# Entry of the second mixture, clock keepers, router banks, GpSimd's queue and two orders of block 3 in a three-block transformer kernel

## The chip, the cores and the metric

The kernel runs on one core of a Trainium2 chip. It is one program that computes three transformer blocks in a row. What counts is its time on the device in microseconds, as the median of several runs. TensorE (PE) runs at one of two clock levels, 1.2 and 2.4 GHz; the profile shows the granted clock of a stretch as a share of the full one, so 0.50 is the lower level throughout. The other engines are VectorE (DVE), ScalarE (ACT), GpSimd (POOL) and SyncE (SP); transfers are issued from the queues of SP, ACT and POOL.

## What is computed

All activations are 512 rows of 1024 (S = 512, D = 1024), fp32. The reference, cut to the parts that the change touches:

```
x = first_block(x, mem, ...)        # mixer, cross attention, small mixture
# second block
merged = g0 * (o_da @ w_da_o) + g1 * (o_wa @ w_wa_o) + g2 * (o_xa @ w_xa_o)
x  = x + merged @ w_out
h2 = rmsnorm(x, ffn_norm_g)
aff  = softmax(h2 @ w_router)                    # 512 x 16
g, i = top_k(aff.T, 64)                          # each expert takes 64 rows
xe   = h2[i]
ye   = (silu(xe @ w_gate) * (xe @ w_up)) @ w_down * g    # 16 experts of 2048
x    = x + scatter_add(ye, i)
x    = rmsnorm(x, final_norm_g)
# third block
q, k, v, q_lat, kv_lat, k_rope, g_a, g_b = split(x @ w_in)
y_a = neighbourhood_attention_2d(q, k, v, rpb) @ w_branch_na    # 8 rows of 64 columns
y_b = latent_attention(q_lat, kv_lat, k_rope, ...) @ w_branch_mla
m   = (sigmoid(g_a) * y_a + sigmoid(g_b) * y_b) @ w_out
x   = layer_norm(a * x + m); x = layer_norm(a * x + swiglu(x))
```

## The kernel before, in words

The rows of the activations are four tiles of 128 (a = 0 to 3). Dense products of fp32 operands are made from two halves each: `split` (L227 on ScalarE, L230 on VectorE) makes wh and wl from the raw weights, and each pair of tiles takes three products (high-high, high-low, low-high). The order on each engine is fixed when the program is built: a scheduler places the instructions by their due times, and `issue_after` ties some to others. TensorE runs its row strictly in that order. PSUM has four banks called acc, two called pst, and one pair of banks called sc; a product waits until the earlier reader of its bank is done.

**The second block's end.** Four gatings of the last branch (L1320, L1321) write kv on VectorE and GpSimd. Then `out_proj` (L291) multiplies merged by w_out, in two passes over pairs of tiles, (0, 1) and (2, 3), each with four acc banks. Ahead of it, h is loaded again from memory by four transfers on ScalarE's queue (L1587). When a pair is done, `add_h` (L320) adds to h, and for each tile `moe2_tile` runs: the rows are normed (L901, L905), transposed (L442) and copied, and `router` (L912) makes 16 logits, in the sc bank. Exp (L1615) reads them there; then a transposition (L1619) brings the probabilities into aff, 16 rows of 512.

**The second mixture's entry.** Eight rounds of MAX8 and MATCH_REPLACE8 on VectorE (L1632, L1633) pick 64 rows for each expert. After each, `keep_warm` lets TensorE multiply the eight maxima (L200) and then, in the first six rounds, three times the 128-column identity (L202). A scan (L1639) turns the picks into positions pos, which are transposed (L1645) and compared with a row of indices to a one-hot oh (L1656). `gather` (L1664) multiplies xh by oh, k by k for the first pair of experts. Each expert then multiplies its 64 rows by the gate and up weights (L1701), transposes the result (L1726) and multiplies by the down weights (L1738). For each pair of experts, four spreading products (L1708, two instructions each in the trace) copy the pair's rows of pos and aff over the partitions, from which the scatter matrix is made. The weights arrive by SP's queue, 1 MB each, into a ring of buffers; a transfer waits until the products that read its buffer before are done. Some of the first up weights go to other rooms (L1680).

**Block 3.** The dense product of V (L376) is copied out by VectorE (L1810), written to memory (vd, L1811) and read back as eight windows vw (L1830); rv, the position biases, are read by L1839. All of these stand on ScalarE's queue. Then Q and K follow (L428), the neighbourhood attention with its value products (L1876), and the latent attention, `mla_part`: for each pair of heads, transposes of Q and K (L1961), and then four parts of 128 rows each, with two scores products (L1968), a softmax (ScalarE L477, VectorE L485), transposes of e (L442), copies eT by VectorE (L445) and ScalarE (L447), and value products (L1980). `stagger` interleaves the parts: each part's scores are issued one or two parts ahead of its transposes and values.

## Time and profile before

| | us |
|---|---|
| median of three runs | 3352.58 |
| the runs | 3346.15 to 3354.76 |
| the profiled execution | 3355.08 |
| its span, first to last instruction | 3353.2 |

The span is 1.9 us shorter than the profiled execution; durations are taken from this execution. The mean granted clock is 0.983. TensorE is busy for 94% of the span, VectorE 49%, ScalarE 39%, GpSimd 4%. The stages, roughly: 0 to 900 us the first block, 900 to 1525 the second block's mixer, 1525 to 1575 its output projection, 1575 to 1612 the mixture's entry, 1612 to 2540 the sixteen experts, then block 3: V, Q and K to 2630, the neighbourhood attention to 2720, its branch and the latents to 2807, the latent attention to 2881, and the feed-forward to the end. A row of a timeline shows the start, the length, the engine and its operation, xcount where equal ones follow each other, and in brackets the idle time ahead of it with what ended it.

### The profile page before, as it was taken

Reading aid. Unit: us, or ns where it says so; the run is one execution under the profiler, and the core shown is the slowest. Engines: PE = TensorE matmul, PEld = TensorE weight load, DVE = VectorE, ACT = ScalarE, POOL = GpSimd, SP = SyncE. Lnnn points to the kernel's source line nnn. Section 1 sums busy time; section 2 is a strip of 40 time slices with the busy share of each in tenths; the row PEclk is TensorE's granted clock in tenths of the full one; section 3 lists DMA queues with packets and bytes.
Section 4 is the critical chain, followed back from the end, with each engine's and each line's share of the span. In section 5 each row is a group of like instructions: output and inputs, shape, how many; then the busy total and the mean of one; then the engine's idle time right before and its main releaser. Section 6 shows DMA issues by size and latency. Waiting matters only on the chain.

```text
span 3353.2 us, 41283 instructions
## 1 busy us (share of the span) xinstructions
PE 3168.3 (94%) x15456; PEld 2062.4 (62%) x15456; DVE 1632.4 (49%) x3520; ACT 1291.2 (39%) x2662; POOL 130.9 (4%) x128
## 2 busy tenths in 40 slices
PE   8999989998989999999999999899888999999998
PEld 6778766667758777677534333322225685788886
DVE  5557799987364444856211111011105546573356
ACT  6335568876354354654000000000003444452244
POOL 0010110001000000000000000000000000000000
PEclk9999989999999999999899999999999999999999
DMA  5115489975112122125799999999995220132243
GB/s 174 67 66 157 173 305 382 370 282 177 63 38 88 63 66 88 39 89 199 315 420 426 427 427 427 427 427 427 427 427 205 72 95 26 63 114 90 81 170 138
DMA packets 196554, 713.96 MB, mean 213 GB/s; under 512 B 20144, under 2 KB 28096, under 8 KB 147584
## 3 DMA queue, kind: packets, MB, share of 16 engines
q1 hardware_dynamic: 173888, 668.38, 51.4%
q10 hardware_dynamic: 19520, 32.43, 3.1%
q0 software_dynamic: 2944, 10.49, 1.0%
q8 instruction: 123, 2.02, 0.2%
q14 instruction: 79, 0.65, 0.1%
HBM read 693.68 MB, written 17.56 MB: 212 GB/s over the span
## 4 chain that ended last, share of the span: by engine, by line
PE 69%; DMA 15%; DVE 8%; ACT 4%; issue 2%; POOL 1%; ACTq 0%; POOLq 0%; SPq 0%; DVEq 0%
PE acc L428 23%; PE acc L291 7%; PE acc L1701 6%; PE acc L1103 5%; PE acc L1295 5%; DMA xl<-in_w_exp_up_dram 3%; DMA rawx<-in_w_exp_gate_dram 3%; PE acc L1738 3%; PE acc L1125 3%; DMA rawx<-in_w_exp_down_dram 2%; DMA xl<-in_w_exp_down_dram 2%; PE sc L1664 2%; PE acc L376 2%; PE pst L442 2%; DVE wl L230 2%
## 5 line engine op out<-in xcount | busy, mean ns | idle before, releaser
L230 DVE TENSOR_TENSOR wl<-raw,wh 128x512 fp32r<-128x512 f32 (+3 forms) x910 | 606.0, 682 | 578.6 <-ACT wh L227 528.9
L227 ACT CAST wh<-raw 128x512 fp32r<-128x512 f32 (+3 forms) x910 | 546.5, 612 | 717.1 <-PE acc L428 475.1
L428 PE MATMUL acc<-xh,wh 128*128 128x512 f32 x1072 | 426.5, 398 | 7.2 <-ACT wh L227 5.2
L428 PE MATMUL acc<-xl,wh 128*128 128x512 f32 x1072 | 424.5, 396 | 0.0
L428 PE MATMUL acc<-xh,wl 128*128 128x512 f32 x1072 | 423.1, 395 | 0.0
L1701 PE MATMUL acc<-rawx,xe 128*64 128x512 f32 x1256 | 293.1, 601 | 28.1 <-DMA rawx<-in_w_exp_up_dram 20.4
L428 PEld LDWEIGHTS acc<-xh,wh 128*128 128x128 f32 x1072 | 202.4, 189 | 57.1 <-ACT wh L227 7.8
L428 PEld LDWEIGHTS acc<-xh,wl 128*128 128x128 f32 x1072 | 202.5, 189 | 47.0 <-issue 6.7
L428 PEld LDWEIGHTS acc<-xl,wh 128*128 128x128 f32 x1072 | 202.7, 189 | 44.2 <-issue 5.6
L1701 PEld LDWEIGHTS acc<-rawx,xe 128*64 128x64 f32 x1256 | 84.4, 137 | 227.5 <-issue 149.8
L1738 PE MATMUL acc<-rawx,wh 128*64 128x512 f32 x640 | 145.9, 598 | 10.6 <-DMA rawx<-in_w_exp_down_dram 10.6
L291 PE MATMUL acc<-wl,xsh 128*128 128x512 f32 x336 | 133.8, 398 | 4.8 <-DVE wl L230 4.7
L216 POOL TENSOR_TENSOR pw_r<-pw_v,halfneg 128x1 f32<-128x1 f32 (+2 forms) x64 | 59.1, 924 | 2008.2 <-DVE pw_v L215 1990.6
L291 PE MATMUL acc<-wh,xsl 128*128 128x512 f32 x336 | 132.9, 396 | 0.0
L291 PE MATMUL acc<-wh,xsh 128*128 128x512 f32 x336 | 128.9, 392 | 0.0
L1701 PE MATMUL acc<-raw,xe 128*64 128x512 f32 x512 | 118.5, 597 | 8.4 <-DMA raw<-in_w_exp_gate_dram 8.4
L1720 DVE SCALAR_TENSOR_TENSOR wl<-wl,acc 128x512 f32<-128x512 f32 x32 | 22.0, 687 | 203.6 <-PE acc L1701 203.6
L1727 ACT COPY wh<-pst 128x512 f32<-128x512 f32 x32 | 18.8, 586 | 259.8 <-PE pst L1726 259.7
L477 ACT ACTIVATE e<-e,smx 128x512 f32<-128x512 f32 (+3 forms) x160 | 98.9, 619 | 50.2 <-DVE smx L475 36.4
L1103 PE MATMUL acc<-wh,xeh 128*96 128x512 f32 x256 | 103.7, 406 | 0.7 <-ACT xeh L227 0.7
L1738 PEld LDWEIGHTS acc<-rawx,wh 128*64 128x64 f32 x640 | 42.7, 136 | 99.2 <-issue 70.7
L1103 PE MATMUL acc<-wl,xeh 128*96 128x512 f32 x256 | 103.5, 404 | 0.1
(537 smaller groups left out, 5475.1 us busy)
## 6 DMA issues: line engine op xcount, KB each, us to landing
rawx<-in_w_exp_up_dram SPq DMA_DIRECT2D x80, 1024.0 KB
rawx<-in_w_exp_down_dram SPq DMA_DIRECT2D x80, 1024.0 KB
rawx<-in_w_exp_gate_dram SPq DMA_DIRECT2D x77, 1024.0 KB
raw<-in_w_in_dram SPq DMA_DIRECT2D x58, 1024.0 KB
raw<-in_w_exp_gate_dram SPq DMA_DIRECT2D x34, 1024.0 KB
raw<-in_w_exp_down_dram SPq DMA_DIRECT2D x32, 1024.0 KB
raw<-in_w_exp_up_dram SPq DMA_DIRECT2D x30, 1024.0 KB
raw<-in_w_ffn_out_dram SPq DMA_DIRECT2D x22, 1024.0 KB
```

The costliest lines, as they stand in the source:

```text
L227: nc.scalar.copy(hi, src)
L230: nc.vector.tensor_sub(lo, src, hi.bitcast(F32))
L291: nc.tensor.matmul(acc[a, hf], l[:, js], r, start=(k == 0 and q == 0), stop=(k == nk - 1 and q == 2))
L376: self.nc.tensor.matmul(acc[a], l[:, k, js], r[:, :n], start=(k == 0 and q == 0), stop=(k == nk - 1 and q == 2))
L428: nc.tensor.matmul(outs[j], l, r, start=(kk == 0 and q == 0), stop=(kk == nk - 1 and q == 2))
L442: nc.tensor.transpose(pt[:, k * P:(k + 1) * P], src[:, (b + k) * P:(b + k + 1) * P], self.ident)
L477: nc.scalar.activation(es[i], src[i], AF.Exp, bias=nm[:, i:i + 1], scale=sc[i], accum_out=l[:, i:i + 1])
L1103: nc.tensor.matmul(ps, l[:, k], r, start=(k == 0 and q == 0), stop=(k == 7 and q == 2))
L1125: nc.tensor.matmul(py[hf], l[:, k], r, start=(k == 0 and q == 0), stop=(k == 3 and q == 2))
L1295: nc.tensor.matmul(acc[j], l[:, js], r, start=(k == 0 and q == 0), stop=(k == nk - 1 and q == 2))
L1701: nc.tensor.matmul(acc[f // 2][f % 2 * 64:(f % 2 + 1) * 64], cur[:, k, es], raw[f], start=(k == 0), stop=(k == 7))
L1738: nc.tensor.matmul(py[hf * 64:(hf + 1) * 64], uT[ab][:, kk, c * 64:(c + 1) * 64], raw[:, d, hf * 512:(hf + 1) * 512], start=(i + d == 0), ...
```

## The change

The change does the following.

- Clock keepers: `keep_busy` takes the place of `keep_warm` in the mixture's entry. Its filling products are bf16, 128 by 512, of an identity that is cast once (identb). There are four behind router 2, six behind router 3, four behind the last transposition of the probabilities, three in each of the eight top-k rounds and five at the comparison behind them. They are tied by `issue_after`.
- Router banks: with 16 columns, `router` takes an acc bank instead of sc.
- The row scaling of xs (L905) moves behind Exp in `moe2_tile`; in the first mixture it stays where it was, written in `moe1_tile`.
- The spreading products are tied behind the last product of the gate.
- The loads of h, the writes of vd and the reads of vw and rv go to GpSimd's queue.
- Block 3: V is copied into rooms of the later attention (ne, neT); the weights of V and Q are requested first, those of K go into the room of merged, which is now one tile, m.
- Latent attention: `weave` takes the place of `stagger`; the two scores products of a part are issued apart from each other, and the second, as well as the value products, is tied behind other parts' work in the last three head pairs.
- One eviction of the first mixer (fq) moves from ScalarE to VectorE.

The diff, cut to its core:

```diff
+    def keep_busy(self, x, n, behind=None):
+        ps = self.acc()
+        if x is not None:
+            behind = self.nc.tensor.matmul(ps[:, :x.shape[1]], self.ident[:16], x, start=True, stop=True).ins
+        b = self.identb[:, :P]
+        with self.tc.issue_after(behind):
+            for _ in range(n):
+                self.nc.tensor.matmul(ps, b, b.unsqueeze(1).to_broadcast([P, 4, P]), start=True, stop=True)
...
-                nc.scalar.activation(fq[j], ps, AF.Copy, scale=0.125)
+                nc.vector.tensor_scalar(fq[j], ps, 0.125, None, op0=OP.mult)
...
-        pl = self.sc()[:, 0, :n]
+        pl = self.sc()[:, 0, :n] if n == 20 else self.acc()[:, :n]
...
-            nc.scalar.dma_start(self.h[:, a], self.res_d[a * P:(a + 1) * P, :])
+            nc.gpsimd.dma_start(self.h[:, a], self.res_d[a * P:(a + 1) * P, :])
...
         pl = self.router(xt, 16)
+        if a > 1:
+            self.keep_busy(None, 2 * a, self.routed)
...
         nc.scalar.activation(L, pl, AF.Exp, scale=r, bias=st[:, 1:2], accum_out=st[:, 2:3])
+        nc.scalar.activation(self.hn[:, a], self.hn[:, a], AF.Copy, scale=r)
...
+        if a == 3:
+            self.keep_busy(None, 4, mm.ins)
...
-                self.keep_warm(m8[:16], 3 if i < 6 else 0)
+                self.keep_busy(m8[:16], 3)
...
             nc.vector.tensor_scalar(wk[:16], wk[:16], 0.0, None, op0=OP.is_lt)
+            self.keep_busy(wk[:16, :8], 5)
...
-                    for b, src in ((bp, pos), (bw, aff)):
-                        for d in range(2):
-                            nc.tensor.matmul(b[d * 64:(d + 1) * 64],
+                    with tc.issue_after(gated):
+                        for b, src in ((bp, pos), (bw, aff)):
+                            for d in range(2):
+                                nc.tensor.matmul(b[d * 64:(d + 1) * 64],
...
-            nc.scalar.dma_start(vd[a * P:(a + 1) * P, :], t)
-        self.dense_tiles(W, 8, 1024, 512, xh, xl, ev_v)
+            nc.gpsimd.dma_start(vd[a * P:(a + 1) * P, :], t)
+        raws = {c: [self.raw_group(W, kg, 4, c, 512) for kg in (0, 4)] for c in (1024, 0)}
+        for kg in (0, 4):
+            nc.sync.dma_start(room[:, kg:kg + 4], W[kg * P:(kg + 4) * P, 512:1024].rearrange("(g p) n -> p g n", p=P))
+        raws[512] = [room[:, kg:kg + 4] for kg in (0, 4)]
+        self.dense_tiles(W, 8, 1024, 512, xh, xl, ev_v, raws=raws[1024])
...
-        stagger((mla_part(hp, qt) for hp in range(1, 4) for qt in range(4)), 2)
+        weave([mla_part(hp, qt) for hp in range(1, 4) for qt in range(4)], 2, True)
```

In the changed file L301 is the product of `out_proj`, L452 the transposes, L921 the router, L212 and L208 the keepers, L1664 the transposition of pos, L1683 the gather, L1720 gate and up, L1730 the spreading products, L1748 the transposes ahead of down, L1997 the scores and L2015 the values of the latent attention, L1635 that of the probabilities.

TensorE between the two tile pairs of `out_proj`, before:

```order
L442 MATMUL pst<-c_ident,xh 128x128 x4
L912 MATMUL sc<-rw_8578,gate 128x16 x4
L291 MATMUL acc<-wl,xsh 128x512
L291 MATMUL acc<-wh,xsl 128x512
L291 MATMUL acc<-wh,xsh 128x512
L442 MATMUL pst<-c_ident,xh 128x128 x4
L291 MATMUL acc<-wl,xsh 128x512
L912 MATMUL sc<-rw_8578,gate 128x16 x4
```

The same place after:

```order
L452 MATMUL pst<-c_ident,xh 128x128 x4
L921 MATMUL acc<-rw_8578,gate 128x16 x4
L452 MATMUL pst<-c_ident,xh 128x128 x4
L921 MATMUL acc<-rw_8578,gate 128x16 x4
L452 MATMUL pst<-c_ident,xh 128x128 x8
L921 MATMUL acc<-rw_8578,gate 128x16 x4
L301 MATMUL acc<-wh,xsh 128x512
```

The products of the second pair, which stood between transposes and routers, now begin behind three half routers and all the transposes.

TensorE at the entry of the mixture, from the transposition of pos to the gate, before (names: rawx and raw are weights, xe the gathered rows):

```order
L1645 MATMUL pst<-c_ident,pos 128x16 x4
L1708 MATMUL pst<-pos,c_ident 64x512 x2
L1708 MATMUL pst<-aff,c_ident 64x512
L1664 MATMUL sc<-oh,xh 128x128 x4
L1708 MATMUL pst<-aff,c_ident 64x512
L1701 MATMUL acc<-rawx,xe 64x512 x4
L1664 MATMUL sc<-oh,xh 128x128 x4
```

The same place after, with the last keeper at its head:

```order
L212 MATMUL acc<-identb 128x512
L1664 MATMUL pst<-c_ident,pos 128x16 x4
L1683 MATMUL sc<-oh,xh 128x128 x4
L1720 MATMUL acc<-rawx,xe 64x512 x4
L1683 MATMUL sc<-oh,xh 128x128 x4
```

And where the spreading products of the first pair of experts stand after, on the same engine, behind the last products of expert 0's up weights:

```order
L1720 MATMUL acc<-yp,xe 64x512 x2
L1730 MATMUL pst<-pos,c_ident 64x512 x2
L1730 MATMUL pst<-aff,c_ident 64x512 x2
L1683 MATMUL sc<-oh,xh 128x128 x4
L1748 MATMUL pst<-c_ident,wl 128x128 x4
```

They moved from between the transposition of pos and the gate to between the up products and the transposes ahead of down.

TensorE in the latent attention, at the first part of the second head pair, before:

```order
L1968 MATMUL sc<-mkT,mqT 128x512 x2
L442 MATMUL pst<-c_ident,e 128x128 x8
L1980 MATMUL acc<-eT,mv 64x128
L1968 MATMUL acc<-mkT,mqT 128x512
L1980 MATMUL acc<-eT,mv 64x128 x7
L1968 MATMUL acc<-mkT,mqT 128x512
L442 MATMUL pst<-c_ident,e 128x128 x8
```

The same place after:

```order
L1997 MATMUL sc<-mkT,mqT 128x512
L452 MATMUL pst<-c_ident,e 128x128 x8
L1997 MATMUL sc<-mkT,mqT 128x512
L2015 MATMUL acc<-eT,mv 64x128 x8
L1997 MATMUL acc<-mkT,mqT 128x512
L452 MATMUL pst<-c_ident,e 128x128 x8
```

The second scores product of a part moved between the transposes of an older part and its value products.

## Rows read from the trace of the kernel before

**Rows 1.** Stages: window, length, busy time by engine, clock, DMA share, GB/s.

```profile
1525.00:1549.00 24.00, 23.78 (x100) 19.51 (x101) 16.86 (x29) 12.59 (x25) 0.00 (x0) 0.93 0.51 213
1592.00:1603.00 11.00, 11.00 (x43) 9.76 (x43) 10.21 (x22) 0.00 (x0) 0.00 (x0) 0.50 1.02 428
1608.00:1616.00 8.00, 8.00 (x20) 3.02 (x20) 1.04 (x2) 0.59 (x1) 0.00 (x0) 0.50 0.00 0
1612.00:1653.00 41.00, 41.00 (x196) 17.75 (x196) 5.06 (x9) 3.13 (x8) 0.00 (x0) 0.94 0.77 295
1760.00:2486.00 726.00, 673.03 (x2996) 232.45 (x2994) 91.38 (x134) 40.63 (x69) 0.00 (x0) 1.00 1.01 427
2138.00:2148.00 10.00, 7.03 (x32) 1.80 (x28) 0.49 (x1) 0.00 (x0) 0.00 (x0) 1.00 1.01 424
2820.00:2830.00 10.00, 8.80 (x33) 4.86 (x31) 4.25 (x10) 2.69 (x8) 0.00 (x0) 0.56 0.00 0
2830.00:2880.00 50.00, 43.60 (x310) 27.12 (x312) 29.15 (x62) 23.85 (x62) 0.00 (x0) 1.00 0.00 1
```

**Rows 2.** Waits of SP's queue, 1560 to 1700: total us, times, longest us.

```profile
SPq L1734 <- PE acc L1701: 43.7, 12, 24.9
```

**Rows 3.** Timeline of TensorE at the entry: start us, length us, operation.

```profile
1582.87 3.49 PE L912 MATMUL sc<-rw,gate 128*128 128x16 f32 x16 [1.39 <-ACT L L1615]
...
1604.71 1.97 PE L1708 MATMUL pst<-pos,c_ident 16*64 16x512 f32 x4
...
1608.31 2.08 PE L1664 MATMUL sc<-oh,xh 128*128 128x128 f32 x8
1610.31 1.96 PE L1708 MATMUL pst<-aff,c_ident 16*64 16x512 f32 x2
1612.21 3.68 PE L1701 MATMUL acc<-rawx,xe 128*64 128x512 f32 x8
...
1620.25 1.16 PE L1664 MATMUL sc<-oh,xh 128*128 128x128 f32 x8
```

**Rows 4.** Timeline of VectorE at the entry, first and last round of eight.

```profile
1589.09 0.68 DVE L1632 MAX8 m<-aff 16x8 f32<-16x512 f32 x1
...
1599.81 0.68 DVE L1632 MAX8 m<-nx 16x8 f32<-16x512 f32 x1
...
1605.07 0.69 DVE L1656 TENSOR_TENSOR oh<-c_iota,pn 128x512 f32<-128x512 f32 x1
```

**Rows 5.** Timeline of TensorE in the output projection.

```profile
1525.22 0.80 PE L291 MATMUL acc<-wl,xsh 128*128 128x512 f32 x1 [2.32 <-DVE wl L230]
...
1548.51 0.49 PE L291 MATMUL acc<-wl,xsh 128*128 128x512 f32 x1
...
1555.72 0.39 PE L291 MATMUL acc<-wl,xsh 128*128 128x512 f32 x1
1555.95 0.40 PE L291 MATMUL acc<-wh,xsl 128*128 128x512 f32 x1
```

**Rows 6.** GpSimd's indirect loads: durations ns min/median/max, first and last start us.

```profile
L1132 POOL DMA_INDIRECT xe<-hn_d,rt x16: 909/1313/2398, 425.8 to 636.5; - x16
```

**Rows 7.** Timeline of ScalarE at block 3's entry.

```profile
2585.51 0.62 ACT L227 CAST wh<-raw 128x512 fp32r<-128x512 f32 x1 [10.02 <-DMA vw<-vd]
```

**Rows 8.** Timeline of TensorE at the same place.

```profile
2594.37 0.80 PE L428 MATMUL acc<-xh,wh 128*128 128x512 f32 x1 [4.88 <-ACT wh L227]
...
2600.08 0.46 PE L428 MATMUL acc<-xl,wh 128*128 128x512 f32 x1
```

**Rows 9.** Transfers of GpSimd's queue: count, median us from issue to landing.

```profile
xe<-hn_d,rt POOLq DMA_INDIRECT x16, 8.2
```

**Rows 10.** The neighbourhood attention's value products: durations ns, first and last start us.

```profile
L1876 PE MATMUL pst<-neT,vw x128: 272/273/324, 2630.6 to 2684.8; 128*64 128x128 f32 x128
```

**Rows 11.** Waits of TensorE, 2800 to 2885: total us, times, longest us.

```profile
PE acc L1980 <- ACT eT L447: 7.1, 10, 0.7
```

**Rows 12.** Timeline of TensorE in the latent attention.

```profile
2847.02 1.12 PE L1968 MATMUL acc<-mkT,mqT 96*128 96x512 f32 x2
```

More of the change, by code (lines that the diff above doesn't have):

```diff
@@ L1599, in moe2_open @@
         self.aff = R.tile([P, S], F32, name="aff")
-        self.pad = R.tile([P, 72], F32, name="rpad")
+        self.identb = R.tile([P, 144], BF, name="identb")
+        nc.vector.tensor_copy(self.identb[:, :P], self.ident)
         self.hn = self.xp.tile([P, 8, S], F32R, name="xh").bitcast(F32).rearrange("p (a k) t -> p a (k t)", a=4)
@@ L1700, in moe2 @@
                         for f in range(4):
-                            nc.tensor.matmul(acc[f // 2][f % 2 * 64:(f % 2 + 1) * 64], cur[:, k, es], raw[f],
-                                             start=(k == 0), stop=(k == 7))
+                            mm = nc.tensor.matmul(acc[f // 2][f % 2 * 64:(f % 2 + 1) * 64], cur[:, k, es], raw[f],
+                                                  start=(k == 0), stop=(k == 7))
+                    if not pg:
+                        gated = mm.ins
                     pg.append(acc)
@@ L1800, in mixer3 @@
         o_ml = [B.tile([P, S], F32, name=f"oml{i}") for i in range(4)]
-        merged = [B.tile([P, S], F32, name=f"m{i}") for i in range(8)]
+        room = B.tile([P, 8, S], F32, name="m")
+        merged = [room[:, i] for i in range(8)]
         self.g8 = B
@@ L1808, in ev_v @@
         def ev_v(a, ps):
[L1809 removed]
+            t = (N.tile([P, 2, 256], F32, name="ne", bufs=2).rearrange("p i k -> p (i k)") if a % 2 else
+                 N.tile([P, 4, P], F32, name="neT", bufs=2).rearrange("p k t -> p (k t)"))
             nc.vector.tensor_copy(t, ps)
[L1811 to L1813 removed]
+            nc.gpsimd.dma_start(vd[a * P:(a + 1) * P, :], t)
[4 more added lines that the diff above has]
+        self.dense_tiles(W, 8, 1024, 512, xh, xl, ev_v, raws=raws[1024])
         anti = self.const("anti", N)
@@ L1966, in mla_part, with scores @@
             sp = self.sc() if hp == 0 or qt % 2 == 0 else [self.acc(), self.acc()]
-            for b in range(2):
-                nc.tensor.matmul(sp[b] if isinstance(sp, list) else sp[:, b], T[2 * b][:96, qt * P:(qt + 1) * P],
-                                 T[2 * b + 1][:96], start=True, stop=True)
+            def scores(b):
+                return nc.tensor.matmul(sp[b] if isinstance(sp, list) else sp[:, b],
+                                        T[2 * b][:96, qt * P:(qt + 1) * P], T[2 * b + 1][:96], start=True, stop=True)
+            scores(0)
+            yield
+            with behind():
+                last[0] = scores(1).ins
             e = H.tile([P, 2, S], F32, name="e", bufs=3)
@@ L1974, in mla_part @@
             for b in range(2):
-                self.transposes(eT[:, b], e[:, b], 4, eng="a" if b else "v")
+                last[0] = self.transposes(eT[:, b], e[:, b], 4, eng="a" if b else "v")
+            yield
             po = self.pst() if hp == 0 else self.acc()
@@ L1981, in values, with behind, weave @@
                                         start=(kt == 0), stop=(kt == 3))
-            self.together([lambda kt=kt, b=b: values(kt, b) for kt in range(4) for b in (1, 0)])
+            with behind():
+                self.together([lambda kt=kt, b=b: values(kt, b) for kt in range(4) for b in (1, 0)])
             nc.scalar.copy(o_ml[hp][:, qt * P:(qt + 1) * P], po[:, :P])
         heads = {}
-        stagger(mla_part(0, qt) for qt in range(4))
+        last = [None, False]
+        def behind():
+            return tc.issue_after(last[0]) if last[1] else ExitStack()
+        def weave(parts, depth, tied):
+            open_ = []
+            for g in parts:
+                o = open_.pop(0) if len(open_) == depth else None
+                next(g)
+                last[1] = tied and o is not None
+                if o is None or not tied:
+                    next(g)
+                if o is not None:
+                    next(o)
+                    if tied:
+                        next(g)
+                    next(o, None)
+                open_.append(g)
+            last[1] = False
+            for g in open_:
+                next(g)
+                next(g, None)
+        weave([mla_part(0, qt) for qt in range(4)], 1, False)
         for hf in range(2):
```

26 lines of the change are left out of this document (13 added, 13 removed).

## The prediction, made before the changed kernel ran

> **What bounds the kernel now.** The table by stage comes first, since one bound does not hold for the whole span [rows 1]. From 1760 to 2486 us the DMA engines are full (share 1.01, 427 GB/s) while PE works 673 of 726 us: the sixteen large experts of the second mixture are bound by their weights, so PE time saved there is worth nothing. What counts is when that stream starts to run without a break. Between 1608 and 1616 us DMA moves 0 GB/s, and PE runs at half clock (granted 0.50). In the other stages that the change touches PE is the bound: 100% busy, or waiting for one named engine.
>
> Why DMA stands still is read from the queue's own waits [rows 2]: the loads of down weights wait for products of the gate (L1701), 24.9 us at the longest. All weight buffers are full, and the first comes free only when the first eight products of the gate, begun at 1612.21, have run [rows 3]. So PE's way to that row is the path. Ahead of it stand, in PE's own row [rows 3]: the last router (L912 x16, which waits 1.39 us for a score bank that Exp still reads), the top-k rounds, and then eight spreading products (L1708), six of them from 1604.71 on, ahead of the first gather (L1664), and two behind it at 1610.31. The gather's one-hot was ready at 1605.07 + 0.69 = 1605.76 [rows 4]; the gather began at 1608.31.
>
> **The entry of the mixture.** *Spreading products behind the gate.* The gather can start 2.4 us earlier (1608.31 to about 1605.9). Between gather and gate stand 1.9 us of spreading products; PE then waits instead for the copy of the gathered tile. No row shows that wait bare; it is above 0 and not over the 1.9, since the gate followed the spreading products at once. I take half, so 1.0 us is won and 3.4 us together, at either clock. The eight instructions now stand behind the products of expert 0's up weights, still ahead of its down products; their 3.6 + 1.9 = 5.5 us, halved at full clock to 2.7, can delay the release of buffers there. The first expert has PE 41 of 41 us busy with DMA at 0.77 [rows 1], so this is not hidden; I charge 1 us (0 to 2.7), nearer to 0, because PE catches up: from 1760 on it has slack. In later pairs PE idles 53 us in 726 for weights, and the same move costs nothing.
>
> *Router banks.* The routers of 16 columns leave the score bank for an accumulator bank. The 1.39 us wait goes, but four keepers now stand there (about 0.9 us at full clock by the step below, 1.7 at half), so at best 0.5 us is won.
>
> *Keepers of full width.* The old ones are 128 columns of fp32; PE is busy 11.00 of 11 us from 1592 to 1603 and the granted clock stays at 0.50 [rows 1]. It comes back only behind the 512-column products that begin at 1612.21: the gather takes 2.08 us at 1608.31 and 1.16 at 1620.25 [rows 3]. The new keepers are 512-column products, four after router 2, ten around router 3, three in each top-k round and five after the last. A round is (1599.81 - 1589.09) / 7 = 1.53 us of VectorE [rows 4]; three keepers at full clock take 0.7 of it, with their first product some 0.9, 6 parts in 10, and from 2138 to 2148 the clock stays at 1.00 with PE busy 7.03 of 10 [rows 1]. Then the last router takes half of its 3.49 us (1.7 won), the gather 1.16 in place of 2.08, the first eight gate products about half of 3.68 (1.8) [rows 3]. With about 0.6 us of queue for the five keepers ahead of the last transpose, this is 0.5 + 1.7 + 0.9 + 1.8 - 0.6 = 4.3 us, beside the 3.4 of the order. VectorE's chain is unchanged. If the clock is not up, the keepers of a round take 1.3 us and their first product some 0.5, 0.3 more than the round; over eight rounds, with some of the last five behind, PE lags by up to 2.7 us, and the entry gains 3.4 - 2.7 to 3.4, some 1 to 3 us.
>
> By the Trainium skill, TensorE: Matmul & The Clock Gate, Part 1, section "What's actually happening", activity as such releases the throttle. The row of 1592 to 1603 us speaks against reading it plainly: full activity, half clock. By the plain rule the new keepers do no more than the old, and the sum is that of the first rival.
>
> The entry: 3.4 + 4.3 - 1 = 6.7, and I take **-7** (-10 to -1). DMA resumes by as much earlier, and the weights behind it are fixed in number.
>
> **The output projection ahead of it.** *Its start.* PE waits 2.32 us for the low half of the first weights (VectorE L230), which stands behind the last gatings; then it runs below full clock: 0.93 over 24 us [rows 1, 5], 1.7 us lost. Now the first split stands ahead of the gatings, and the loads of h leave ScalarE's queue for GpSimd's. The accumulator banks still have to be read first, one VectorE instruction on 128x512 ahead of the first (0.69 by the size of [rows 4]). I take **-3** (0 to -4). On GpSimd's queue these four loads stand between multiplications of kv, 1.31 us of issue each by GpSimd's indirect loads, the nearest row [rows 6]. That kv is the second half of the operand, which comes up after four of eight steps, some 10 us later, and h is first needed when the first pair of tiles is done, about 1548 [rows 5]: both are covered.
>
> *Its middle.* Between the tile pairs 19 products of the second pair, 1548.51 to 1555.95, fill the waits of the transposes and routers [rows 5]; one is 0.23 us, so 4.3 us of cover. With routers in accumulator banks the second pair finds its banks only after the additions to h and Exp; in the new order three routers' halves and all transposes come ahead of the first product of the second pair. PE then waits for the copies: from 0 (the rest of the chain gets shorter by as much) to 4.3 us. I take **+2.5**, nearer to the upper end, since in the new order no product is left between them.
>
> **Block 3's entry.** ScalarE's queue holds the gathers of the windowed V (vw). One of them waits for V to land, and the cast of the next weights waits 10.02 us behind it [rows 7]; PE ends up idle for 4.88 us at 2594.37, and its next 13 products step by (2600.08 - 2594.37) / 13 = 0.44 us in place of 0.23 [rows 5, 8]: 4.9 + 13 x 0.21 = 7.6 us, with a smaller wait ahead of it about 8. The change moves vd, vw and rv to GpSimd's queue, which has nothing else to do in this stage; the K weights come early into other room. What is late next is vw itself: the wait for the last V block begins at 2585.51 - 10.02 = 2575.5 [rows 7]; a write and four gathers at 1.31 us of issue and 8.2 us to land twice [rows 6, 9] are done by about 2599. Its first reader, L1876, runs at 2630.6 [rows 10], some 8 us earlier after the change, at 2622: 23 us of room. I take **-8** (-8.5 to 0).
>
> **Latent attention.** PE waits ten times, 7.1 us together, between transposes of e and their value products, for ScalarE's copy eT [rows 11]. The new order puts the second scores product of the next part there, about 1 us of work (the row of one shows 1.12 [rows 12]), against 0.7 us of wait. Eight to ten of these waits are covered; at the last two parts nothing is left to put there. Scores come later by one transposition, but the softmax has two parts' time. **-5** (-10 to +1: the low end if the stretch at half clock from 2820 to 2830 shrinks as well, the other if the reduction of the late scores holds VectorE's copy). The eviction of fq from ScalarE to VectorE in the first mixer is four instructions of the size of rows 7's cast (0.62 us) beside full PE: 0.
>
> **Sum.** -7 - 3 + 2.5 - 8 - 5 = -20.5 us. Against the profiled execution (3355.1 us, 3353.2 of it span) that is 3334.6; against the median of 3352.6 it is 3332.1. The forecast is stated on the median: **3332 us**.
>
> **Rivals.**
> *Clock stays down at the entry.* Keepers wait for each round's first product and leave gaps; the old ones did nothing for the clock. Against it: the products behind which it did come back, at the gate and at 2600.08 [rows 8], have 512 columns too. The entry gives 2 in place of 7: 3337. Chance 0.22.
> *The first expert gives it back.* PE is full to 1760 and DMA stands at 0.77 there, so buffers are released at PE's pace; with the spreading products and the middle of the projection at their upper ends (-2 and +2), and a DMA stream that only starts 3 us earlier, the second mixture nets 0: 3352.6 - 13 = 3339.6, or 3340. Chance 0.13.
> *GpSimd's queue is late.* Its indirect loads take from 0.91 to 2.40 us to issue, 1.31 at the median, beside a VectorE that works [rows 6]. Two writes and four gathers use up the 23 us of room when each takes 23 / 6 = 3.8 us more than 1.31, some 5.1 us, twice the longest seen. At 6.5 us each, vw is 8 us late, and block 3's gain is gone: 3340. Chance 0.05. The Trainium skill, SBUF — State Buffer, section "SBUF: two separate sides", gives such a mechanism: a DMA issued by GpSimd waits while VectorE runs an operation that takes the port they share; no run here shows it.
> *The attention loses the clock (slower).* At the start of the last three head pairs PE waits for scores banks, and the clock falls: 0.56 in 2820 to 2830, while the 50 us behind are at 1.00 with 43.6 us busy [rows 1]. The new order begins with the same wait. If its mix of transposes and short products does not bring the clock back at 2829, the 50 us take about 35 us more (half clock nearly doubles 43.6 us; 6.4 us of idle absorb a part). It decides itself at one point, the first part of the second head pair. Sum -15.5 + 35: 3372. Against: the waits that lie between are fewer than before. Chance 0.03.
> *The scheduler undoes it.* Row scalings still stand ahead of Exp of tile 2, and if PE's time is set by other chains in each place: 3350. Chance 0.05.
>
> **How the numbers follow.** Forecast 0.52, rivals 0.22, 0.13, 0.05, 0.03, 0.05. The range is from 3320 (all gains at their far ends: -10 - 4 + 0 - 8.5 - 10 = -32.5) to 3347: it takes in the first three rivals and leaves out the last two and the tails. About 0.3%, 10 us, is what a measurement of this kernel can tell from no change: faster means below 3342.5. The forecast and the first rival are there nearly whole, the second and third in somewhat over half: 0.83. Within 0.3%: 0.13. Slower: 0.04.
>
> **What would show it.** The first gate product starts at about 1605 in place of 1612.2, with a granted clock of 1.00 from about 1590; no stretch of 0 GB/s longer than 3 us near 1608; the spreading products stand behind the up products. PE has no wait over 1 us near 2590 and no clock below 0.9 there. The ten eT waits are down to two to four. PE idles up to 2.5 us near 1550. Wrong it would be if the expert phase ends less than 4 us earlier relative to the start of the entry, or if a wait for vw or rv shows in the neighbourhood attention.

## The result and the profile after

The changed kernel takes 3331.62 us, the median of four runs (3330.38 to 3334.32); the kernel before, on the same chip, 3352.76 us (four runs). The ratio is 0.9941, with an interval of 0.9924 to 0.9959: faster by 0.6%, 21 us. The forecast was 3332 us. The profiled execution took 3330.38 us, so it is 24.7 us shorter than the profiled one of before (3355.08).

The page of the changed kernel gives the span and the busy time of the engines.

```profile
span 3328.6 us, 41332 instructions
PE 3153.2 (95%) x15465; PEld 2052.6 (62%) x15465; DVE 1636.8 (49%) x3525; ACT 1289.8 (39%) x2658; POOL 143.5 (4%) x152
```

The same line of the page of before:

```profile
PE 3168.3 (94%) x15456; PEld 2062.4 (62%) x15456; DVE 1632.4 (49%) x3520; ACT 1291.2 (39%) x2662; POOL 130.9 (4%) x128
```

The number of products is nearly the same. TensorE's busy time falls by 15.1 us, its idle time by the other 9.5: a product at half clock counts as busy for longer, so part of what the clock costs stands in the busy time.

To see where it went, both traces are cut at the same products of TensorE, and each piece is measured from the cut before it. That is needed here: the time at which `out_proj` is reached, about 1520 us, differed by 6 us (1519.6 to 1525.6) between ten profiled executions whose instructions up to there are the same (those of the changed kernel and of all experiments but one that moved the loads of h).

| piece | forecast, us | before | after | difference |
|---|---|---|---|---|
| to the start of `out_proj` | 0 | 1522.05 | 1520.20 | -1.9 |
| its first tile pair | -3 | 26.10 | 22.91 | -3.2 |
| its rest ("middle") | +2.5 | 27.92 | 35.86 | **+7.9** |
| its end to the first product of the gate | -5.9 | 36.14 | 29.21 | -6.9 |
| first product of the gate to the last scatter product | -0.8 (-1.8 for the first eight products of the gate, +1 charged) | 930.7 | 931.3 | +0.6 |
| last scatter product to the last neighbourhood value | -8 | 141.9 | 135.9 | -6.0 |
| from there to the first acc scores of the latent attention | 0 | 126.9 | 125.8 | -1.1 |
| latent attention, to the last value product | -5 | 69.0 | 55.0 | **-14.0** |

The sum of the last column is -24.6. That is 3.6 us more than the medians differ by: the profiled execution of before lies 2.3 us above its median here, that of the changed kernel 1.2 below. Two rows are far from the forecast, and they partly cancel: the middle of `out_proj` lost 5.4 us more than was priced, and the latent attention won 9 us more. The table by stretch (length, then busy time of each engine with its instructions, then granted clock, DMA share, GB/s) shows the middle in the changed kernel:

```profile
1541.00:1543.00 2.00, 2.00 (x10) 1.37 (x8) 1.97 (x5) 0.83 (x3) 0.00 (x0) 1.00 0.00 0
1543.00:1545.00 2.00, 1.29 (x11) 1.01 (x10) 2.00 (x4) 2.00 (x4) 0.00 (x0) 1.00 0.00 0
1545.00:1547.00 2.00, 1.22 (x11) 0.98 (x11) 1.51 (x4) 2.00 (x5) 0.57 (x1) 0.98 0.03 8
1547.00:1549.00 2.00, 2.00 (x11) 2.00 (x11) 1.42 (x6) 0.58 (x1) 0.56 (x1) 0.50 0.00 0
...
1557.00:1559.00 2.00, 2.00 (x6) 1.54 (x6) 1.18 (x4) 0.52 (x3) 0.00 (x0) 0.50 0.00 0
1559.00:1561.00 2.00, 2.00 (x7) 1.41 (x6) 0.68 (x3) 1.03 (x2) 0.00 (x0) 0.61 0.00 0
```

and TensorE's timeline of the same place (start, length, operation, count, and the wait ahead of it) shows why:

```profile
1542.68 0.39 PE L301 MATMUL acc<-wh,xsl 128*128 128x512 f32 x1
1543.11 0.63 PE L452 MATMUL pst<-c_ident,xh 128*128 128x128 f32 x4
1544.41 1.07 PE L921 MATMUL acc<-rw,gate 128*128 128x16 f32 x8 [0.67 <-ACT gate L457]
1545.33 0.63 PE L452 MATMUL pst<-c_ident,xh 128*128 128x128 f32 x4
1546.74 1.75 PE L921 MATMUL acc<-rw,gate 128*128 128x16 f32 x8 [0.78 <-DVE gate L455]
...
1552.41 0.63 PE L301 MATMUL acc<-wl,xsh 128*128 128x512 f32 x1
```

In [rows 5] the products of the second pair stand between transposes and routers here. Now they are gone from there, as the forecast said, and TensorE waits 0.67 + 0.78 = 1.45 us. What it did not say: behind these waits the granted clock falls to 0.50 and stays there from 1547 to about 1560.5 us. 13.5 us at half clock are 6.7 us of lost work, and a product is 0.63 long in place of 0.39. 1.45 + 6.7 = 8.2, against 7.9 in the table.

At the entry, the same view and the same timeline answer [rows 1] and [rows 3]:

```profile
1575.00:1590.00 15.00, 12.90 (x81) 9.55 (x80) 8.41 (x23) 6.18 (x12) 1.48 (x2) 1.00 0.81 264
1590.00:1600.00 10.00, 7.25 (x33) 3.12 (x31) 9.31 (x21) 0.00 (x0) 0.00 (x0) 1.00 0.99 397
1600.00:1608.00 8.00, 5.33 (x29) 2.99 (x29) 5.93 (x12) 0.00 (x0) 0.00 (x0) 1.00 0.78 330
1608.00:1612.00 4.00, 3.82 (x10) 1.02 (x11) 0.13 (x1) 0.00 (x0) 0.00 (x0) 0.57 0.00 0
1612.00:1620.00 8.00, 8.00 (x44) 4.00 (x43) 0.29 (x1) 0.27 (x1) 0.00 (x0) 1.00 0.73 262
```

```profile
1605.18 0.41 PE L1664 MATMUL pst<-c_ident,pos 16*128 16x16 f32 x4 [0.78 <-DVE pos L1661]
1606.64 1.16 PE L1683 MATMUL sc<-oh,xh 128*128 128x128 f32 x8 [1.04 <-DVE oh L1675]
1608.18 3.55 PE L1720 MATMUL acc<-rawx,xe 128*64 128x512 f32 x8 [0.38 <-DVE xe L1687]
```

The clock is up from 1575 to 1608, the gather takes 1.16 us instead of 2.08, and no spreading product stands ahead of the gate. But TensorE then waits 0.78, 1.04 and 0.38 us, and the clock falls once more: the first eight products of the gate take 3.55 us, hardly less than the 3.68 of [rows 3], and DMA stands at 0 GB/s from 1608 to 1612.

In block 3, GpSimd's timeline shows the moved transfers: what is shown is the time of each issue on its queue.

```profile
2562.37 2.75 POOL L1858 DMA_DIRECT2D vw<-vd  x4 [2.33 <-DMA vd<-ne]
2565.11 0.59 POOL L1835 DMA_DIRECT2D vd<-neT  x1
2570.44 0.56 POOL L1835 DMA_DIRECT2D vd<-ne  x1 [4.74 <-DVE ne L1834]
2579.12 2.73 POOL L1858 DMA_DIRECT2D vw<-vd  x4 [8.12 <-DMA vd<-ne]
```

The wait for V to land is still there, 8.12 us, but nothing that TensorE needs is queued behind it. The waits of TensorE from 2530 to 2690 us (who waits for whom, total, times, longest) no longer have a row of the Q and K products; one of 1.4 us in V's products (L386), for the low half xl of the input rows, is new. In [rows 8] it was 4.88 us at one place.

```profile
PE acc L386 <- DVE xl L240: 1.4, 1, 1.4
PE pst L1769 <- DVE h L1772: 0.7, 1, 0.7
```

In the latent attention, the waits for eT, ten in [rows 11], are two:

```profile
PE acc L2015 <- ACT eT L457: 2.1, 2, 1.3
PE sc L1997 <- ACT e L488: 1.8, 1, 1.8
```

### The profile page after: what moved, and what is told of

Its sections match the earlier page's. It is cut to its first block, busy times and chain, and to the rows that moved or that the text cites. A ratio compares the mean times of both kernels' runs of the same rounds, so it can differ in the third digit from the quotient of the medians.

```text
span 3328.6 us, 41332 instructions
## 1 busy us (share of the span) xinstructions
PE 3153.2 (95%) x15465; PEld 2052.6 (62%) x15465; DVE 1636.8 (49%) x3525; ACT 1289.8 (39%) x2658; POOL 143.5 (4%) x152
## 4 chain that ended last, share of the span: by engine, by line
PE 54%; DMA 12%; DVE 6%; ACT 3%; issue 1%; POOL 1%; ACTq 0%; POOLq 0%; SPq 0%; DVEq 0%
PE acc L438 20%; PE acc L1720 8%; PE acc L301 5%; PE acc L1306 5%; PE acc L1760 4%; DMA xl<-in_w_exp_up_dram 3%; DMA rawx<-in_w_exp_gate_dram 3%; DMA xl<-in_w_exp_down_dram 3%; PE sc L1683 2%; DMA rawx<-in_w_exp_down_dram 2%; PE pst L1769 2%; ACT e L488 2%; PE pst L452 1%; DMA rawx<-in_w_exp_up_dram 1%; PE acc L386 1%
## 5 line engine op out<-in xcount | busy, mean ns | idle before, releaser
L240 DVE TENSOR_TENSOR wl<-raw,wh 128x512 fp32r<-128x512 f32 (+1 forms) x902 | 601.0, 683 | 556.7 <-ACT wh L237 507.8
L237 ACT CAST wh<-raw 128x512 fp32r<-128x512 f32 (+1 forms) x902 | 542.4, 612 | 696.3 <-PE acc L438 468.6
L1720 PE MATMUL acc<-rawx,xe 128*64 128x512 f32 x1256 | 290.3, 600 | 28.5 <-DMA rawx<-in_w_exp_up_dram 20.2
L1720 PEld LDWEIGHTS acc<-rawx,xe 128*64 128x64 f32 x1256 | 85.4, 137 | 223.5 <-issue 145.2
L301 PE MATMUL acc<-wl,xsh 128*128 128x512 f32 x336 | 133.8, 398 | 3.0 <-DVE wl L240 2.9
L301 PE MATMUL acc<-wh,xsl 128*128 128x512 f32 x336 | 133.3, 397 | 0.0
L1741 DVE SCALAR_TENSOR_TENSOR wl<-wl,acc 128x512 f32<-128x512 f32 x32 | 22.0, 688 | 223.5 <-ACT wl L1740 223.5
L1740 ACT ACTIVATE wl<-acc 128x512 f32<-128x512 f32 x32 | 19.1, 597 | 287.4 <-PE acc L1720 287.4
L301 PE MATMUL acc<-wh,xsh 128*128 128x512 f32 x336 | 130.1, 396 | 0.0
L1720 PE MATMUL acc<-raw,xe 128*64 128x512 f32 x512 | 118.8, 598 | 8.5 <-DMA raw<-in_w_exp_gate_dram 8.5
L1742 DVE SCALAR_TENSOR_TENSOR wl<-wl,acc 128x512 f32<-128x512 f32 x32 | 22.0, 688 | 190.5 <-PE acc L1720 190.5
```

The source lines that it names most:

```text
L237: nc.scalar.copy(hi, src)
L240: nc.vector.tensor_sub(lo, src, hi.bitcast(F32))
L301: nc.tensor.matmul(acc[a, hf], l[:, js], r, start=(k == 0 and q == 0), stop=(k == nk - 1 and q == 2))
L1720: mm = nc.tensor.matmul(acc[f // 2][f % 2 * 64:(f % 2 + 1) * 64], cur[:, k, es], raw[f], start=(k == 0), stop=(k == 7))
```

## The experiments

Each edit is made on the changed kernel. Times are medians; ratios are against the kernel before. The experiments were timed on three chips, each time beside the kernel before (medians of 3349.56 to 3351.32 us), so a difference of 1 or 2 us between two of them is not to be read.

**Score bank again for the first tile pair.** Routers 0 and 1 go back to the sc bank, 2 and 3 stay in acc.

```diff
-    def router(self, xt, n):
+    def router(self, xt, n, sc=False):
-        pl = self.sc()[:, 0, :n] if n == 20 else self.acc()[:, :n]
+        pl = self.sc()[:, 0, :n] if sc or n == 20 else self.acc()[:, :n]
-        pl = self.router(xt, 16)
+        pl = self.router(xt, 16, a < 2)
```

> The changed kernel, with the routers of row tiles 0 and 1 back in the score bank; those of tiles 2 and 3 stay in accumulator banks. Theory 1 (the banks of the first two routers take the second pair's products away from the waits, PE idles 1.45 us and its clock falls for 13.5 us): no stretch at 0.50 between 1543 and 1561, the output projection ends 8 us earlier (about 1571 in place of 1579). As DMA runs nearly full from 1585 to 1606 and stands still only some 5 us, the kernel gains less: 3326 us (-4 to -8). Rival (the row scaling that moved behind Exp, or the loads of h, made the gap): the middle stays as it is, 3331 to 3332.

3323.65 us (3322.81 to 3327.22), ratio 0.9913 (0.9895 to 0.9931). The middle takes 27.36 us, as before the change, and the table by stretch has TensorE full at full clock:

```profile
1545.00:1547.00 2.00, 2.00 (x12) 1.60 (x11) 2.00 (x4) 1.78 (x3) 0.00 (x0) 1.00 0.00 0
1547.00:1549.00 2.00, 2.00 (x16) 1.76 (x16) 2.00 (x6) 2.00 (x5) 0.94 (x1) 1.00 0.03 8
```

So the +7.9 comes from the banks of the first two routers, and it is lost time, not work moved. A repeat gave 3323.64 us (3319.41 to 3325.88), ratio 0.9921 (0.9907 to 0.9934):

> The version with the first two routers back in the score bank, timed again in five rounds beside the next one on the same chip. It settles whether the changed kernel can be beaten: 3324 (0.992 of before), against 0.994 for the changed kernel.

The repeat shows something else. In the first run the clock fell between 1575 and 1590 us, in the second, with the same instructions, it did not. The stretch in the first run:

```profile
1575.00:1590.00 15.00, 13.47 (x61) 9.35 (x60) 5.88 (x20) 5.05 (x11) 1.48 (x2) 0.66 0.70 233
```

The same stretch in the repeat:

```profile
1575.00:1590.00 15.00, 11.90 (x69) 6.57 (x67) 10.45 (x29) 2.49 (x6) 0.03 (x1) 1.00 0.94 357
```

From the end of `out_proj` to the gate it took 33.61 us in the first, 29.22 in the second.

**Keepers for that gap.** The same edit, with three bf16 keepers in the sc bank behind the first transposes of tiles 2 and 3.

```diff
+            if keep and not b:
+                self.keep_busy(None, keep, mm, self.sc()[:, 0])
...
+        xt, r = self.router_T(a, self.hn[:, a], 3 if a > 1 else 0)
```

> The version with the first two routers in the score bank, and three more keepers behind the first transposes of row tiles 2 and 3, written to the score bank, where PE waits 0.68 us twice. Theory 1 (these waits let the clock fall from 1577 to 1587, which costs 4 to 5 us ahead of the top-k rounds): clock at 1.00 there, first gate product about 3 us earlier, the end 1 to 3 us earlier than 3323.7: 3322. Rival (DMA sets the end by then): no change of the end, 3324.

> The version with the score bank for the first two routers and three more keepers behind the first transposes of row tiles 2 and 3, timed again in five rounds. Theory 1 (its traced end of the expert phase is 3 us earlier, counted from the start of the output projection, so the end moves by as much): 3 us below the version without these keepers, 3321. Rival (DMA or the later stages take it back): the same within 1 us, 3324.

3323.73 us (3321.38 to 3327.16), ratio 0.9925 (0.9909 to 0.9942), and in the repeat 3323.16 us (3320.94 to 3327.43), ratio 0.9918 (0.9905 to 0.9932): the same as without them within 1 us. The pieces from `out_proj`'s end to the gate are 29.86 and 29.22 us. Whether they help when the clock would have fallen, two runs cannot tell.

**All routers in acc, the waits filled.** To learn whether idle time alone brings the clock down, the changed order stays and three keepers follow both transposes of tile 0.

```diff
+            if keep:
+                self.keep_busy(None, keep, mm, self.sc()[:, 0])
...
+        xt, r = self.router_T(a, self.hn[:, a], 3 if a == 0 else 0)
```

> The changed kernel (all 16-column routers in accumulator banks) with three keepers each behind the two transposes of row tile 0, where PE waits 0.67 and 0.78 us in the middle of the output projection. Theory 1 (of 8.1 us lost there 6.7 are the clock, 1.4 the wait): clock stays at 1.00, the middle costs 1.5 to 2 us in place of 8, the projection ends 6 us earlier, and the end comes as close to the run with score banks as its clock behind it allows: 3326. Rival (bank waits as such cost the time): the projection ends as late as in the changed kernel, 3332.

3329.51 us (3326.48 to 3331.13), ratio 0.9937 (0.9921 to 0.9954); the middle takes 32.99 us. By the same table TensorE was hardly idle, and the clock fell all the same:

```profile
1545.00:1547.00 2.00, 1.97 (x15) 1.37 (x13) 1.83 (x4) 2.00 (x5) 0.00 (x0) 1.00 0.04 8
1547.00:1549.00 2.00, 1.86 (x15) 1.24 (x13) 1.68 (x3) 1.90 (x3) 0.57 (x1) 1.00 0.00 0
1549.00:1551.00 2.00, 1.76 (x17) 1.52 (x16) 2.00 (x9) 1.35 (x4) 0.75 (x1) 1.00 0.00 0
1551.00:1553.00 2.00, 2.00 (x9) 1.64 (x9) 0.76 (x3) 0.63 (x1) 0.00 (x0) 0.62 0.11 20
1553.00:1555.00 2.00, 2.00 (x11) 1.90 (x10) 0.00 (x0) 0.00 (x0) 0.00 (x0) 0.50 0.89 324
```

So theory 1 failed in its main point, that the clock stays up. The rival failed as well: the middle is 2.9 us shorter than in the changed kernel, as the clock falls later and is down for about half as long, to 1558 us.

**The loads of h back on ScalarE's queue.** `nc.gpsimd.dma_start(self.h[:, a], ...)` becomes `nc.scalar.dma_start`.

> The changed kernel with the four loads of h back on ScalarE's queue. Theory 1: PE waits about 2.3 us again at the start of the output projection and loses 1 to 2 us of clock: the projection's first pair ends 3.4 us later; the end +1 to +3, as DMA takes a part, 3333. Rival (VectorE's order, with the split ahead of the gatings, did it alone): start unchanged, 3332.

3332.68 us (3330.23 to 3336.71), ratio 0.9945 (0.9925 to 0.9964): no difference in time that this can tell. The start of `out_proj` is back at 26.26 us, with the wait of before, so the -3.2 comes from the queue of h. With the loads in ScalarE's row, VectorE also writes the first low half of w_out (L240) behind the gatings again, at 1526.06 us; in the changed kernel it does so ahead of them, at 1518.10. Queue and order moved together, and no run separates them. But the middle, with the instructions of the changed kernel, takes 29.93 us. The wait at the start:

```profile
PE acc L301 <- DVE wl L240: 2.3, 1, 2.3
```

Two stretches of the middle:

```profile
1549.00:1551.00 2.00, 1.47 (x8) 0.80 (x6) 2.00 (x5) 1.49 (x4) 0.00 (x0) 1.00 0.00 0
1551.00:1553.00 2.00, 1.55 (x12) 1.31 (x12) 1.51 (x4) 2.00 (x4) 0.56 (x1) 1.00 0.04 8
```

The waits stand there as in the changed kernel, and the clock stays at 1.00. So the banks by themselves cost 29.93 - 27.92 = 2.0 us, close to what the forecast gave them (2.5). Why the clock stays up here is open. In all five profiled executions that have this order of products and h on GpSimd's queue it falls in the middle, for some 13.5 us in four of them and 10 in the fifth. In this run it had fallen earlier, behind the wait at the start (0.58 from 1528 to 1532 us). The profiled execution is also the fastest of the four, at a mean clock of 0.990; the others have 0.986 to 0.988, so the median may hold falls that this trace does not show.

**The old keepers.** `keep_warm` comes back in the top-k rounds, the keepers at the routers, the last transposition and the comparison are removed; the spreading products and the banks stay as changed.

```diff
+    def keep_warm(self, x, n):
...
-        if a > 1:
-            self.keep_busy(None, 2 * a, self.routed)
...
-                self.keep_busy(m8[:16], 3)
+                self.keep_warm(m8[:16], 3 if i < 6 else 0)
...
-            self.keep_busy(wk[:16, :8], 5)
```

> The changed kernel with the clock keepers of before (128 columns of fp32, six rounds) and none behind the routers. Theory 1 (full-width keepers hold the clock through the top-k rounds): granted clock 0.50 from about 1584 to 1612, the first gate product 3 to 5 us later counted from the end of the output projection; the end +3 to +4, 3335. Rival (the order alone made the entry shorter): first gate product within 1 us, 3332.

3329.74 us (3328.53 to 3334.55), ratio 0.9944 (0.9928 to 0.9961). The clock is down, as in [rows 1]:

```profile
1590.00:1600.00 10.00, 10.00 (x40) 8.78 (x40) 9.27 (x21) 0.00 (x0) 0.00 (x0) 0.50 0.99 407
1600.00:1608.00 8.00, 5.84 (x26) 5.05 (x27) 4.57 (x8) 0.00 (x0) 0.00 (x0) 0.50 0.68 285
```

and yet the gate comes 29.28 us behind `out_proj`, against 29.21. The pieces say why (from the end of `out_proj` to the first MAX8, then to the one-hot, then to the gate): before 13.0, 16.0, 7.1; changed 11.1, 15.8, 2.3; old keepers 10.1, 16.0, 3.2. The full clock takes 0.9 off the gather. The ten keepers around router 3 delay the first MAX8 by 1.0; most of it is the four ahead of router 3's last products, which end 0.8 us later behind them. (The four keepers behind the last transposition of the probabilities come too late to delay it.) The rounds in between are VectorE's and do not depend on the clock. And the last routers run at full clock without any keeper:

```profile
1583.06 2.75 PE L921 MATMUL acc<-rw,gate 128*128 128x16 f32 x24
```

Before, 16 such products took 3.49 us at half clock, behind the wait of 1.39 us for the score bank [rows 3]. That wait is gone in both versions, so it is the bank, or the order that came with it, and not the keepers, that lets the top-k start earlier; no run separates these two.

**The spreading products set free.** Only the tie behind the gate is removed.

```diff
-                    with tc.issue_after(gated):
-                        for b, src in ((bp, pos), (bw, aff)):
+                    for b, src in ((bp, pos), (bw, aff)):
```

> The changed kernel with the spreading products free again, so that for the first pair of experts six of them stand ahead of the first gather and two behind it. Theory 1 (the prediction's step: they hold up gather and gate, at full clock 5.5 / 2 - 1.4 us of waits that they fill = 1.3 us, with first gate products at half clock as before): +1 to +3, 3334. Rival (in the changed kernel the waits there cost the clock, 2.2 us on the first gate products; with the spreading products in them it stays up): 0 or a gain of 1, 3331.

3329.58 us (3326.13 to 3332.85), ratio 0.9937 (0.9920 to 0.9954). The gate starts 2.3 us later after `out_proj` (31.48), but behind it the transfers run better. The stretch from 1640 to 1660 us in the changed kernel (DMA share and GB/s stand last):

```profile
1640.00:1660.00 20.00, 20.00 (x100) 7.83 (x98) 3.50 (x5) 2.95 (x5) 0.00 (x0) 1.00 0.85 336
```

The same in this one:

```profile
1640.00:1660.00 20.00, 20.00 (x97) 7.40 (x94) 2.76 (x4) 2.37 (x4) 0.00 (x0) 1.00 0.96 364
```

From the gate to the last scatter product it takes 930.1 us, the changed kernel 931.3. So the tie gives 2.3 us up to the gate. Whether it takes 1.2 behind it is not shown: runs with the tie in place need 929.8 to 932.1 us there. The time does not show the difference. The rival fell: the spreading products now fill the waits of 1.04 and 0.38 us (the 0.78 ahead of pos stays), and the clock falls ahead of the gate all the same. Its first eight products, with no wait ahead of them:

```profile
1610.43 3.68 PE L1720 MATMUL acc<-rawx,xe 128*64 128x512 f32 x8
```

**vd, vw and rv back on ScalarE's queue.** Three `nc.gpsimd.dma_start` become `nc.scalar.dma_start`.

> The changed kernel with vd, vw and rv back on ScalarE's queue; the order of the weights' loads and the room for K stay. Theory 1 (casts of weights were held behind the gathers on ScalarE's queue): PE idles some 5 us at about 2590 again and loses 2 to 3 us of clock: +6 to +8, 3338. Rival (the earlier weights alone did it): no wait over 1 us there, 3332.

3337.47 us (3335.09 to 3344.23), ratio 0.9960 (0.9947 to 0.9973): 5.9 us slower than the changed kernel, close to theory 1. In the trace, the piece from the last scatter product to the last neighbourhood value is back at 142.3 us, and the one behind it at 126.9. The largest of TensorE's waits there:

```profile
PE acc L438 <- ACT wh L237: 5.9, 1, 5.9
```

And the row of ScalarE's timeline that causes it; the cast stands behind a read on the same queue:

```profile
2589.36 0.62 ACT L237 CAST wh<-raw 128x512 fp32r<-128x512 f32 x1 [15.63 <-DMA rv<-in_na_rpb_dram]
```

**The old order of the latent attention.** `mla_part` and `stagger` of before are put back.

```diff
-        weave([mla_part(hp, qt) for hp in range(1, 4) for qt in range(4)], 2, True)
+        stagger((mla_part(hp, qt) for hp in range(1, 4) for qt in range(4)), 2)
```

> The changed kernel with the latent attention's part order of before. Theory 1 (one change of order both fills the copies' waits, 5 us, and gives the clock back 6 us earlier at the first part of the second head pair, 5 us, and the rest follows): +14 us, 3345. Rival (the clock's return was an accident of the phase in which the stage began): +5 us, 3337, with the stretch at half clock as short as in the changed kernel.

3341.57 us (3338.62 to 3344.35), ratio 0.9970 (0.9960 to 0.9980): 10 us slower, between theory 1 and the rival, and in the trace the last value product comes 10.7 us later after the last neighbourhood value. All ten waits are back:

```profile
PE acc L2008 <- ACT eT L457: 7.1, 10, 0.7
```

**What beats both.** The changed kernel with the first two routers in the sc bank, about 3323.6 us. Its interval against before (0.9907 to 0.9934 in the repeat) still touches that of the changed kernel (0.9924 to 0.9959), but in all four runs with that edit the middle is 27.4 us and not 35.9, and the last scatter product comes 1010.6 to 1013.7 us after the start of `out_proj`, not 1019.3.

## Why the prediction came out right, and where it was wrong

The time was met to 0.4 us, and that is partly luck: two terms of the sum were off by 5 and 9 us in opposite directions, both for the same omission, a clock that was left out of the term. The interval of the ratio alone is 6 us to either side.

**The middle of the output projection (+2.5 forecast, +7.9 measured).** The step bounded the cost by the cover that is lost, 0 to 4.3 us, and took 2.5. That part held: 1.45 us of waits here, 2.0 us of time in the run with h on ScalarE's queue, where the clock stayed up. What failed is the bound itself: it counted idle time only. Removing 512-column products from between transposes and routers also exposes the clock, 6.7 us here. The score bank for the first pair takes the whole of it away, so the cause lies in these two routers' banks and the order that goes with them. What exactly decides about the fall is not settled. Idle time alone does not: with the waits filled the clock fell though the stretches ahead were 88 to 98% busy, and in the run with h on ScalarE's queue it stayed up with 74 to 78%.

**The entry (-7 forecast).** From the end of `out_proj` to the last scatter product the changed kernel gains 6.3 us: 6.9 to the gate, less 0.6 behind it, where a charge of 1 was put. The sum held, its parts only in half. The order was sized at 3.4; the way from the one-hot to the gate shrank by 4.8, 0.9 of it the gather's clock, so 3.9 is the order (2.3 where the clock is up, by the run with free spreading products). The clock's part was sized at 4.3, and this is the step that failed. The gather gave 0.9 as forecast. The last router's 1.7 was put down to the keepers, but the top-k starts earlier without them too, by 2.9 us, and with them by 1.9. The first eight gate products, sized at 1.8, gave 0.1, because the clock falls again at the gate. The waits just ahead of it do not explain that alone: with free spreading products it fell with only the first of the three left, and in the first run with the score bank it stayed up behind all three:

```profile
1606.44 1.94 PE L1720 MATMUL acc<-rawx,xe 128*64 128x512 f32 x8 [0.38 <-DVE xe L1687]
```

So the new keepers bring nothing at this place. The first rival (clock stays down, entry 2 in place of 7) fell twice: the clock was up, and with the clock down the entry gains the same.

**Does the first expert give it back?** No. From the first gate product to the last scatter product every kernel of this study needs 929.8 to 932.1 us, before 930.7. The end of this phase moves as much as the first gate product does. Since `out_proj` lost 7.9 - 3.2 = 4.7 of the 6.9, the phase ends only 1.55 us earlier, counted from the start of `out_proj`. So what this rival forecast, a second mixture that gains next to nothing, nearly came true, but through the middle of the projection and not through the first expert. One sign of the forecast is missed as well: DMA still stands at 0 GB/s for the 4 us from 1608 to 1612, where at most 3 were expected, as the first gate products run below full clock.

**The start of the output projection (-3).** -3.2; of the wait of 2.32 in [rows 5] 0.5 us is left, and it comes back whole with h on ScalarE's queue.

**Block 3 (-8).** -6.0, with the mechanism as forecast: undoing it costs 5.9 us. The term missed what is late next: a new wait of 1.4 us in V's products for xl. VectorE writes it late, because its row stops ahead of it for bg, the gates' biases, whose load stands on ScalarE's queue:

```profile
2545.28 0.17 DVE L1820 TENSOR_SCALAR bg<-bg 128x16 f32<-128x16 f32 x1 [1.73 <-DMA bg<-in_b_gate_dram]
```

This load was issued at 2539.09, so it took 6.2 us; before, VectorE found it landed within 4.4. The wait for xl (0.8 to 1.5 us) is in every profiled run of the changed kernel and its variants but the one with vd, vw and rv on ScalarE's queue. That the loads moved to GpSimd's queue delay bg is likely by this, but was not tested by itself. The rest, 0.6, was not followed. The rival in which GpSimd's queue is late found nothing: four gathers take 2.75 us to issue, 0.69 each, half of the 1.31 taken from [rows 6], and the last of them is issued at 2581.9, 40 us ahead of its first reader at 2621.6. The stall of GpSimd's DMAs behind VectorE that the Trainium skill, SBUF — State Buffer, section "SBUF: two separate sides", describes does not show in these issues; whether VectorE's operations beside them are of the kind that the page means, the trace does not tell.

**Latent attention (-5).** -14.0. The waits went as forecast, from ten to two, 5.0 us. The clock was left at 0 in the term, though the range let it fall out of the half-clock stretch. First the kernel before, from the first late scores product to the transposes of the next head pair, by when the clock is up, and the part behind:

```profile
2815.43:2830.51 15.08, 13.73 (x43) 7.45 (x43) 7.07 (x16) 4.49 (x12) 0.00 (x0) 0.55 0.00 1
2830.51:2880.74 50.23, 43.98 (x320) 27.49 (x319) 29.15 (x62) 23.34 (x61) 0.00 (x0) 1.00 0.00 1
```

Then the changed kernel, cut in the same way:

```profile
2804.93:2814.19 9.26, 9.26 (x56) 5.60 (x57) 6.68 (x15) 4.07 (x11) 0.00 (x0) 0.82 0.00 0
2814.19:2856.20 42.01, 38.89 (x307) 25.44 (x305) 30.35 (x64) 23.63 (x61) 0.00 (x0) 1.00 0.00 1
```

A clock of 0.55 over 15.08 us loses 6.8 us, 0.82 over 9.26 loses 1.7: 5.1 us. With 5.0 of waits that is 10.1; the remaining 4 lie in busy time. Behind the fall, at the same clock, 175 value products take 14.9 us before, and 162 take 11.2 now. Some 0.9 of that is the 13 products more; the rest is that a group which the wait splits into two starts twice (2 products take 0.43 us and the other 14 1.09, where 16 in one piece take 1.09). With the old order on the changed kernel the loss is 10 to 10.7 us, and its own fall, at 2808 to 2816 us with 0.57, costs 3.4 in place of 6.8. So 10 to 11 of the 14 are the order; the other 3 are how long the clock happened to stay down in the one profiled run of before. The profiled runs bear it out: the clock costs 0 to 1.7 us in this stage in the ten that have the new order, 3.4 and 6.8 in the two that have the old one. The slower rival (the clock stays down) did not come.

**The eviction of fq (0).** Not tried by itself. The -1.9 us ahead of `out_proj` are no evidence for it, since that time varies by 6 us with equal instructions.

## What to carry to other kernels

Where an edit takes wide products out from between short ones, price the granted clock beside the idle time: here a loss of 2 us in waits became one of 8, and a gain of 5 one of 10 or more. Test a filler product by leaving it out: these raised the clock as meant and gave back as much in TensorE's queue. Measure stages from a common product, not from the start of the span, and take the start of a DMA-bound phase as the point to move: what comes behind it stayed within 2 us of 931 whatever was done ahead of it.

## What was not expected of the hardware

- The same kernel loses its clock in one execution and not in another: at the end of `out_proj` a clock of 0.66 over 15 us in one run and 1.00 in its repeat, 4.4 us apart at the gate. In the middle of `out_proj` it fell in all five profiled executions of one order, and not in the sixth, where h is on another queue.
- In the run with filled waits the clock fell to 0.50 though TensorE had been busy 88 to 98% of the stretches ahead, with transposes, 16-column products and bf16 fillers.
- Direct transfers issued by GpSimd took 0.56 to 0.69 us each on its queue beside a working VectorE, well under the 0.91 to 2.40 us of its indirect loads.
